# One attention head of sixteen: turned by TensorE in place of VectorE and GpSimd

## The chip, the cores and the metric

The kernel runs on one core of a Trainium2 chip. The core has a matrix engine (TensorE, PE in the profile; its weight loads are PEld), a vector engine (VectorE, DVE), a scalar engine (ScalarE, ACT), GpSimd (POOL) and a queue engine that issues the transfers (SyncE, SP). Each runs its own instruction stream in order and waits for the others through semaphores. SBUF is the on-chip memory of 128 partitions; PSUM is the small memory that TensorE writes to. The metric is the device time of one execution in microseconds, taken as the median of several runs.

## The reference

Two layers work on 256 tokens of 2048 features in float32. Each layer has a mixing part and a gated MLP with a three-tap convolution. The mixing part makes one large projection of the normalised input, which yields queries, keys and values of two attention mixers and two gates. Mixer A is a windowed attention with 8 query heads and 2 key/value heads and a sink logit per head; mixer B is a neighbourhood attention of 8 heads with a learned bias. Cut to what matters here:

```python
qa, ka, va, qb, kb, vb, ga, gb = split_cols(h @ w_in[l])
qa = rotary_partial(rmsnorm(qa.reshape(B, S, HA, HEAD_DIM), qn_a[l]), pos)
...
s = jnp.einsum('bnqgrd,bnkgd->bgrnqk', qb, kw) * (HEAD_DIM ** -0.5)
...
p = jnp.exp(s - m)
p = p / (jnp.sum(p, axis=-1, keepdims=True) + jnp.exp(snk - m))
o = jnp.einsum('bgrnqk,bnkgd->bnqgrd', p, vw)
```

For every head the kernel holds the probabilities `p` with queries on the partitions (two tiles of 128 queries by 256 keys). The product with the values needs keys on the partitions, so each head's 256 x 256 matrix has to be turned before it.

## The kernel before

**The weight stream.** All weights come in units of 16 blocks of 128 x 128 (1 MB), in an order written out by hand (`block_stream`). Every weight is split into a rounded high half, a cast by ScalarE (L338), and the rest as a low half, a subtraction by VectorE (L339); the activations are split likewise, and TensorE multiplies high by high, high by low and low by high. In the token-major projection that runs here (`tokens`, L456 to L458) a unit holds 24 matmuls of 512 columns. Units come through four raw SBUF buffers, which they share with the weights of the adaLN products (L241, on VectorE), and four half-unit buffers `hl`.

**The background.** After each unit a tick runs (`Stream.tick`, `Paced.tick`): first what was deferred, then the paced jobs. One of these is the attention (`attention`, L972), which in layer 1, the second layer, takes 0.4 steps per tick (`ATT`). A step takes each live head one `yield` further, oldest first, and then starts the next head.

**A head.** `attend` (L712) issues, from one step to the next: scores on TensorE (L718) and softmax (VectorE L721 to L736, ScalarE L730 and L738); the turn; the split of the turned matrix `pT` into high (ScalarE, L473) and low (VectorE, L476); and the product with the values (L758) with its own split into `oA` (L761, L762). A turn is made in one of two ways. *Moved*: VectorE transposes the 32 x 32 blocks inside `p` into scratch rows (L319), and GpSimd copies the 16 blocks to their places (L313); one step later the split reads `p` from SBUF. The scratch rows of head `i` in mixer A are `qTa[:, i - 1 : i + 1]`, the queries of head `i` and of the head before, already used (L945); head 0 has a spare tile. *By TensorE*: two steps after the softmax four transposes of 128 x 128 go into a PSUM tile `tp` (L747 to L750), and the split reads that in the same step. In the moved form the ScalarE half of the split is pinned behind what stands on ScalarE's queue so far (`held`, L474).

`MOVED[l]` (L96) says which heads are moved: none in layer 0, all eight of each mixer in layer 1.

**Neighbours.** The projection runs in nine groups of 512 columns. After a group come the squares of its heads (ScalarE, L643), VectorE's sum (L526), a small power on GpSimd (`rsqrt`, L527, the tile `qrs`), and VectorE's product (L653, the tile `qn`), which in layer 1 is pinned in VectorE's queue (`pinned`). One tick later the rows are turned (`turn`): groups 0, 1, 2 and 8 in the moved way (`MOVED_QK`), the others by eight TensorE transposes (L689) into two PSUM tiles `qtp`, which ScalarE empties (L690). Groups 3 and 6 are the keys of mixer B, 5 and 8 its queries.

**PSUM.** `qtp`, `sc` (scores), `tp`, `po` (product with the values) and two rarer tiles share the pool `ax` of three buffers, in turn; the projections have four of their own.

**Order.** Inside an engine the instructions stand in the order in which the tile framework's planner puts them, by program order and by readiness in its own model; `keep_in_program_order` pins one behind those traced before it.

Of the kernel before, what the change touches and what calls it, by code (L numbers as in the profile page):

```python
# [28 lines left out]
SCALE = HEAD ** -0.5  # L29
# [63 lines left out]

MOVED_QK = [(), (0,1,2,8)]
QK_STEPS = 3
MOVED = [(0,0), (8,8)]  # L96
STEPS = [1, 1]

ADA_ORDER = [[p * KC + k for k in range(KC) for p in ps] for ps in ((0, 1), (2,), (3, 4), (5,))]
# [58 lines left out]
def encoder(ctx: ExitStack, tc: tile.TileContext, a: dict, out: bass.AP):  # L158
# [38 lines left out]
    def place(tag, n, dt, name):  # L197
        return sp.tile([P, n, S], dt, name=name, tag=tag)

    def chunks_of(p, tag, room, name, n):  # L200

        t = p.tile([P, room, 2, S], F32R, name=name, tag=tag)
        return [t[:, i] for i in range(n)]
# [5 lines left out]
    def paired(dt, name):  # L209

        return ev.tile([P, 2, S], dt, name=name, tag="u", bufs=2)[:]
# [487 lines left out]
    def in_halves(src, name, tag, yes):  # L699

        if not yes:
            return (src,)
        hl = at.tile([P, 2 * S], F32R, name=name, tag=tag, bufs=1)[:]
        halves = hl.rearrange("p (i s) -> p i s", i=2) if len(src.shape) == 2 else hl.rearrange("p (i a s) -> p i a s", i=2, a=2)
        split(halves, src)
        return halves[:, 0], halves[:, 1]
# [150 lines left out]
    tables = []  # L857

    def small(l):

        if l == 0:
            tables.append(load(a["maskA"], [P, 2, S], "maskA"))
        once = at.tile([P, 2, S], F32, name=f"once{l}", tag="p", bufs=3)[:, 0]
        cs = once[:, : 4 * HALF].rearrange("p (f t d) -> p f t d", f=2, t=2)
        rg = once[:, 4 * HALF : 8 * HALF].rearrange("p (w d) -> p w d", w=2)
        nc.sync.dma_start(cs, a["cs"])
        nc.sync.dma_start(rg, a["rg"][l])
        gains = load(a["gains"][l], [P, 4], f"gains{l}", lay, tag="gains", bufs=1)
        sink = load(a["sink"][l], [P, HA], f"sink{l}", lay, tag="sink", bufs=1)
        nc.vector.tensor_scalar(out=gains[:, 2:3], in0=gains[:, 2:3], scalar1=SCALE, scalar2=None, op0=ALU.mult)  # L870
        rots = []
        for w in range(2):
            rot = lay.tile([P, 4, 2, HALF], F32, name=f"rot{l}_{w}", tag=f"rot{w}", bufs=1)
            for i, (f, g) in enumerate(((0, 0), (1, 1), (0, 1), (1, 0))):
                nc.vector.tensor_tensor(
                    out=rot[:, i], in0=cs[:, f],
                    in1=rg[:, w, g * HALF : (g + 1) * HALF].unsqueeze(1).broadcast_to([P, 2, HALF]), op=ALU.mult,
                )
            rots.append(rot)

        return gains, sink, rots

    for l in range(L):
# [39 lines left out]
        oA, oB = [], []  # L923

        def head_a(i):
            g = i // (HA // GA)
            if i >= 6:
                oA.append(paired(F32R, f"oA{l}_{i}"))
            elif i % 2 == 0:
                o = place(("y0", "y1", "y2")[i // 2], 4, F32R, f"oA{l}_{i}")  # L930
                oA.extend((o[:, :2], o[:, 2:]))
            q = in_halves(qTa[:, i], f"qA{l}_{i}", "qh", l in SCORES_3)
            if i % (HA // GA) == 0:
                kvs[0] = in_halves(kTa[:, g], f"kA{l}_{g}", "kh", l in SCORES_3)
            k = kvs[0]
            yield
            p = at.tile([P, 2, S], F32, name="p", tag="p", bufs=3)

            def v():
                if i % (HA // GA) == 0:  # L940
                    kvs[1] = in_halves(packs[0][:, 1:4:2, g * HEAD : (g + 1) * HEAD], f"vA{l}_{g}", "vh", True)
                return kvs[1]

            def rows():
                return qTa[:, i - 1 : i + 1] if i else paired(F32, f"spare{l}")  # L945

            yield from attend(
                q, k, v, p, tables[0], SCALE, sink[:, i : i + 1], lambda: oA[i], rows if i < MOVED[l][0] else None
            )

        def head_b(hb):
            b, i = packs[1 + hb // 4], hb % 4
            v = b[:, 4:8].rearrange("p (t a) s -> p t (a s)", t=2)
            p = at.tile([P, 2, S], F32, name="p", tag="p", bufs=3)
            nc.sync.dma_start(p[:], a["bias"][l, hb])
            q = in_halves(b[:, 8 + i], f"qB{l}_{hb}", "qh", l in SCORES_3)
            k = in_halves(b[:, i], f"kB{l}_{hb}", "kh", l in SCORES_3)
            yield
            yield from attend(
                q, k, lambda: in_halves(v[:, :, i * HEAD : (i + 1) * HEAD], f"vB{l}_{hb}", "vh", True), p, p, 1.0, None,  # L960
                lambda: oB_of(hb), (lambda: b[:, i : 9 + i : 8]) if hb < MOVED[l][1] else None,
            )

        def oB_of(hb):
            if hb == 0:
                o = place("a", 12, F32R, f"oB{l}_{hb}")
                oB.extend(o[:, 2 * i : 2 * i + 2] for i in range(6))
            elif hb == 6:
                oB.extend(chunks_of(sp, "b0", 6, f"oB{l}_{hb}", 2))
            return oB[hb]  # L970

        def attention():  # L972

            todo = [(EARLY[l] + i // 4, head_a, i) if l in EARLY else (3, head_a, i) for i in range(HA)] + [(6 + 3 * (i // 4), head_b, i) for i in range(HB)]
            live = []
            while todo or live:
                for head in list(live):
                    if next(head, bg) is bg:
                        live.remove(head)
                        heads[0] += 1  # L980
                if todo and ready[0] >= todo[0][0]:
                    live.append(todo[0][1](todo[0][2]))
                    next(live[-1])
                    todo.pop(0)
                yield
# [19 lines left out]
        for pi, (groups, gates) in enumerate(parts):  # L1005
            last = pi == len(parts) - 1
            for g, part in enumerate(groups):
                have_h(part)
                pss = st.tokens(h, part)
                if pi == max(0, len(parts) - 2) and g == 0:  # L1010
                    gains, sink, rots = small(l)
                dst = packs[g // 3][:, 4 * (g % 3) : 4 * (g % 3) + 4]
                rows = dst.rearrange("p (t a) s -> p t a s", t=2)
# [311 lines left out]
```

## Time and profile before

| what | us |
|---|---|
| median of 3 runs | 2582.84 |
| lowest and highest run | 2577.52, 2583.45 |
| the profiled execution | 2582.28 |
| its span in the profile | 2580.4 |
| TensorE busy in the span | 2542.0 |
| VectorE busy | 2206.3 |
| ScalarE busy | 1452.9 |
| GpSimd busy | 243.5 |

The span runs from the first to the last instruction of the profiled execution; 1.9 us of that execution lie around it. A row of the timeline gives the start and the length in microseconds, the engine, the line, the operation, the tile written and the tiles read, the shapes, and in brackets the idle time of that engine just before and what ended it. A row of the stretches gives the stretch, its length, the busy time and the number of instructions of PE, PEld, DVE, ACT and POOL, then the clock granted to TensorE (1.00 is full), the share of the DMA engines' time and GB/s. The chain of work follows the last instruction back, at each step to what released it; its rows in order of time hold start, length, engine, tile and line.

In the second layer the moved turns lie between 1382 and 1695 us, the only long stretch in which GpSimd has work.

### The profile page before, as it was taken

The numbers are of one execution on the slowest core, as the hardware profiler recorded it, in microseconds if no ns is written. First come the engines' busy times: TensorE is split into PE (matmuls) and PEld (weight loads), VectorE is DVE, ScalarE is ACT, GpSimd is POOL, SyncE is SP. The second block draws the span as 40 slices with busy tenths as digits, with TensorE's granted clock in tenths as the row PEclk, the third lists the DMA queues.
The fourth block names the chain that finished last, engine by engine and source line by source line (L and its number), as shares of the span: only waits on it lengthen the run. The fifth ranks groups of instructions, "written<-read, shape, count | busy, mean of one in ns | idle before, by whom it ended". The sixth has DMA issues, their size and how long they took to land.

```text
span 2580.4 us, 41173 instructions
## 1 busy us (share of the span) xinstructions
PE 2542.0 (99%) x16204; PEld 2343.3 (91%) x16204; DVE 2206.3 (85%) x3177; ACT 1452.9 (56%) x2400; POOL 243.5 (9%) x345
## 2 busy tenths in 40 slices
PE   8999999999999999999999989999999999999999
PEld 7888888899999999999998879999999999999998
DVE  8999998998998899899987778879889987766775
ACT  5445865446654665466565666644576546644663
POOL 0000100000000000000004668710000000000000
PEclk9999999999999999999999999999999999999999
DMA  9998689885788778777767667779847775555554
GB/s 364 356 348 308 256 326 359 338 302 217 267 292 308 259 279 299 288 279 280 284 222 275 259 228 267 274 275 332 302 173 293 292 293 198 207 199 197 206 201 147
DMA packets 102149, 699.84 MB, mean 271 GB/s; under 512 B 12865, under 2 KB 15169, under 8 KB 18113
## 3 DMA queue, kind: packets, MB, share of 16 engines
q1 hardware_dynamic: 101954, 697.20, 72.6%
q8 instruction: 127, 2.08, 0.3%
q14 instruction: 68, 0.56, 0.1%
HBM read 695.06 MB, written 2.10 MB: 270 GB/s over the span
## 4 chain that ended last, share of the span: by engine, by line
PE 75%; DVE 14%; DMA 3%; issue 3%; ACT 3%; POOL 2%; DVEq 0%; POOLq 0%; ACTq 0%; SPq 0%
PE ps L381 31%; PE ps L382 15%; DVE hl L339 5%; PE ps_t L457 5%; PE ps_t L458 5%; PE ps_t L456 5%; PE ps L387 4%; PE ps L385 4%; PE ps L386 4%; DVE aw L241 4%; DMA aw<-in_aw 3%; POOL packA L313 1%; ACT hl L338 1%; PE sc L718 1%; DVE x L1137 1%
## 5 line engine op out<-in xcount | busy, mean ns | idle before, releaser
L339 DVE TENSOR_TENSOR hl<-w,hl 128x1024 fp32r<-128x1024 f32 x928 | 1129.2, 1224 | 231.0 <-ACT hl L338 228.6
L338 ACT CAST hl<-w 128x1024 fp32r<-128x1024 f32 x928 | 965.8, 1049 | 583.0 <-PE ps L382 262.0
L381 PE MATMUL ps<-h,hl 128*128 128x512 f32 x2432 | 796.8, 382 | 0.0
L382 PE MATMUL ps<-h,hl 128*128 128x256 f32 x2432 | 663.1, 273 | 0.0
L381 PEld LDWEIGHTS ps<-h,hl 128*128 128x128 f32 x2432 | 460.2, 189 | 63.6
L382 PEld LDWEIGHTS ps<-h,hl 128*128 128x128 f32 x2432 | 467.6, 192 | 0.0
L241 DVE CUSTOM_DVE_ANT_0 aw<-aw,cact,ab 128x2048 f32<-128x2048 f32 x189 | 443.8, 2349 | 15.2 <-DMA aw<-in_aw 14.6
L457 PE MATMUL ps_t<-hl,h 128*128 128x512 f32 x832 | 318.6, 383 | 6.1 <-DVE hl L339 5.9
L456 PE MATMUL ps_t<-hl,h 128*128 128x512 f32 x832 | 315.3, 384 | 4.8 <-ACT hl L338 2.5
L458 PE MATMUL ps_t<-hl,h 128*128 128x512 f32 x832 | 316.6, 381 | 0.0
L457 PEld LDWEIGHTS ps_t<-hl,h 128*128 128x128 f32 x832 | 158.2, 190 | 32.7 <-DVE hl L339 11.2
L456 PEld LDWEIGHTS ps_t<-hl,h 128*128 128x128 f32 x832 | 157.6, 190 | 29.2 <-ACT hl L338 4.5
L458 PEld LDWEIGHTS ps_t<-hl,h 128*128 128x128 f32 x832 | 158.3, 190 | 22.0
L381 PE MATMUL ps<-act_o,hl 128*128 128x512 f32 x512 | 170.5, 382 | 0.0
L1164 DVE SCALAR_TENSOR_TENSOR u<-both,cw,u 128x255 f32<-128x255 f32 x304 | 146.0, 480 | 3.8
L387 PE MATMUL ps<-merged,hl 128*128 128x256 f32 x512 | 141.0, 276 | 6.4 <-DVE hl L339 6.4
L385 PE MATMUL ps<-merged,hl 128*128 128x256 f32 x512 | 141.0, 276 | 0.8 <-ACT hl L338 0.5
L386 PE MATMUL ps<-merged,hl 128*128 128x256 f32 x512 | 140.8, 275 | 0.0
L382 PE MATMUL ps<-act_o,hl 128*128 128x256 f32 x512 | 139.6, 273 | 0.0
L1186 ACT COPY both<-ps 128x256 f32<-128x256 f32 x152 | 56.3, 371 | 123.8 <-PE ps L382 122.8
L1137 DVE SCALAR_TENSOR_TENSOR x<-ps,mod,x 128x256 f32<-128x256 f32 x224 | 105.0, 480 | 21.6 <-PE ps L382 19.5
L381 PE MATMUL ps<-act_y,hl 128*128 128x512 f32 x352 | 118.3, 382 | 0.0
(266 smaller groups left out, 4632.4 us busy)
## 6 DMA issues: line engine op xcount, KB each, us to landing
w<-in_ws SPq DMA_DIRECT2D x463, 1024.0 KB, 4.9
aw<-in_aw SPq DMA_DIRECT2D x189, 1024.0 KB, 4.9
p<-in_bias SPq DMA_DIRECT2D x16, 256.0 KB, 4.4
x<-in_xT SPq DMA_DIRECT2D x4, 512.0 KB, 5.6
aw_o<-in_aw SPq DMA_DIRECT2D x2, 1024.0 KB, 12.4
out<-x SPq DMA_DIRECT2D x16, 128.0 KB, 2.5
w<-in_ws SPq DMA_DIRECT2D x2, 512.0 KB, 11.8
aw_b<-in_aw SPq DMA_DIRECT2D x1, 1024.0 KB, 18.1
```

The costliest lines, as they stand in the source:

```text
L241: product = nc.vector.tensor_tensor_reduce(out=raw[:], in0=raw[:], in1=cact[:], scale=1.0, scalar=ab[:, i : i + 1], op0=ALU.mult, op1=ALU. ...
L338: nc.scalar.copy(hl[:, 0], r)
L339: nc.vector.tensor_tensor(out=hl[:, 1], in0=r, in1=hl[:, 0].bitcast(F32), op=ALU.subtract)
L381: nc.tensor.matmul(ps[:], hi, act.both, start=first, stop=False)
L382: nc.tensor.matmul(ps[:, :S], lo, act.high, start=False, stop=last)
L385: nc.tensor.matmul(out, hi, act[0], start=first, stop=False)
L386: nc.tensor.matmul(ps[:, :S], hi, act[1], start=False, stop=False)
L387: nc.tensor.matmul(out, lo, act[0], start=False, stop=last)
L456: nc.tensor.matmul(ps[:], xh, hi, start=kc == kcs[0], stop=False)
L457: nc.tensor.matmul(ps[:], xh, lo, start=False, stop=False)
L458: nc.tensor.matmul(ps[:], xl, hi, start=False, stop=kc == kcs[-1])
L1164: nc.vector.scalar_tensor_tensor(out=u[:, to], in0=ps[:, of], scalar=w[:, j : j + 1], in1=u[:, to], op0=ALU.mult, op1=ALU.add)
```

## The change

The bound "the first n heads" becomes a set of heads for each layer and mixer, and head index 2 of mixer A is not in layer 1's set:

```diff
-MOVED = [(0,0), (8,8)]
+MOVED = [((), ()), ((0, 1, 3, 4, 5, 6, 7), range(8))]
...
-                q, k, v, p, tables[0], SCALE, sink[:, i : i + 1], lambda: oA[i], rows if i < MOVED[l][0] else None
+                q, k, v, p, tables[0], SCALE, sink[:, i : i + 1], lambda: oA[i], rows if i in MOVED[l][0] else None
...
-                lambda: oB_of(hb), (lambda: b[:, i : 9 + i : 8]) if hb < MOVED[l][1] else None,
+                lambda: oB_of(hb), (lambda: b[:, i : 9 + i : 8]) if hb in MOVED[l][1] else None,
```

That head then takes the other branch of `attend`, which layer 0 takes for all its heads:

```python
        yield
        if rows is not None:
            turned_blocks(p[:], rows(), 2)
            for _ in range(STEPS[sink is None]):
                yield
            tp = p
        else:
            yield
            tp = ax.tile([P, 2, S], F32, name="tp", tag="ax")
            for k in range(2):
                for t in range(2):
                    nc.tensor.transpose(tp[:, k, t * P : (t + 1) * P], p[:, t, k * P : (k + 1) * P], ident[:])
        pT = at.tile([P, 2, 2, S], F32R, name="pT", tag="pT", bufs=1)
        split(pT, tp[:], held=rows is not None)
```

## The prediction

> **What bounds the kernel now.** I read the page's head first, for the span and the busy shares, and then the chain's shares by engine.
>
> ```profile
> span 2580.4 us, 41173 instructions
> PE 2542.0 (99%) x16204; PEld 2343.3 (91%) x16204; DVE 2206.3 (85%) x3177; ACT 1452.9 (56%) x2400; POOL 243.5 (9%) x345
> PE 75%; DVE 14%; DMA 3%; issue 3%; ACT 3%; POOL 2%; DVEq 0%; POOLq 0%; ACTq 0%; SPq 0%
> ```
>
> TensorE is busy for 2542.0 of 2580.4 us, so it is the bound, and only 38.4 us of it are idle. An edit off TensorE pays only where one of those gaps closes; an edit that adds TensorE work costs its full length wherever there is no gap. The next view is the stretches around the third head, with TensorE's busy time as the second number and the granted clock (PEclk) as the third from the end.
>
> ```profile
> 1480.00:1500.00 20.00, 17.22 (x86) 14.96 (x85) 11.42 (x13) 10.90 (x29) 14.58 (x26) 1.00 0.55 211
> 1500.00:1520.00 20.00, 15.70 (x75) 13.57 (x74) 16.14 (x33) 14.02 (x40) 10.26 (x21) 0.91 0.57 211
> 1520.00:1540.00 20.00, 20.00 (x104) 17.76 (x103) 16.83 (x25) 12.41 (x21) 10.42 (x16) 1.00 0.72 263
> ```
>
> From 1480 to 1520 us TensorE is idle for 2.78 + 4.30 = 7.08 us, almost a fifth of its idle time in the whole program, and the clock falls. From 1520 on it is full. The third head is turned exactly here. TensorE's timeline (start, length, and in brackets the idle time before it) and the chain in order of time say which work is late:
>
> ```profile
> 1498.93 0.48 PE L457 MATMUL ps_t<-hl,h 128*128 128x512 f32 x1 [2.78 <-DVE hl L339]
> 1504.00 1.04 PE L689 MATMUL qtp<-ident,qn 128*128 128x128 f32 x8
> 1504.79 0.91 PE L758 MATMUL po<-pT,vA 128*128 128x256 f32 x6
> 1510.23 1.23 PE L718 MATMUL sc<-kA,qA 128*128 128x256 f32 x6 [4.30 <-ACT packB L690]
> ```
> ```profile
> 1510.23 1.23 PE sc L718 x6
> 1511.46 0.43 PE ps_t L457
> ...
> 1514.02 0.34 PE ps_t L457
> ...
> 1528.84 0.67 PE sc L718 x6
> 1534.69 0.87 PE qtp L689 x8
> ```
>
> The first gap waits for VectorE's low halves of a weight unit (L339), the second for ScalarE to empty the PSUM tiles of group 5's turned queries (L690). After the second gap the same six score matmuls take 1.23 us where they take 0.67 a step later, and the seven matmuls from 1511.46 to 1514.36 (1514.02 + 0.34) take 2.90 us where seven of 0.22 take 1.54. That is 0.56 + 1.36 = 1.92 us lost to the clock.
>
> Why are VectorE and ScalarE late? VectorE, GpSimd and ScalarE, in this order:
>
> ```profile
> 1483.96 0.71 DVE L319 STREAM_TRANSPOSE packA<-p 128x512 f32<-128x512 f32 x1 [2.50 <-POOL p L313]
> 1488.01 0.25 DVE L526 TENSOR_SCALAR qss<-qss 128x8 f32<-128x8 f32 x1
> 1496.46 1.29 DVE L653 TENSOR_TENSOR qn<-ps_t,qrs 128x512 f32<-128x512 f32 x2 [5.85 <-POOL qrs L527]
> 1499.93 0.42 DVE L762 TENSOR_TENSOR oA<-po,oA 128x256 fp32r<-128x256 f32 x1
> 1505.89 0.16 DVE L736 RECIPROCAL ri<-den 128x2 f32<-128x2 f32 x1
> ```
> ```profile
> 1475.59 8.34 POOL L313 COPY p<-packA 32x128 f32<-32x128 f32 x16 [5.84 <-DVE packA L319]
> 1484.74 9.97 POOL L313 COPY p<-packA 32x128 f32<-32x128 f32 x16 [0.81 <-DVE packA L319]
> 1494.79 1.64 POOL L527 TENSOR_TENSOR qrs<-qss,mhalf 128x8 f32<-128x8 f32 x1
> ```
> ```profile
> 1481.57 1.03 ACT L338 CAST hl<-w 128x1024 fp32r<-128x1024 f32 x1
> 1490.62 1.99 ACT L338 CAST hl<-w 128x1024 fp32r<-128x1024 f32 x2 [3.87 <-DVE hl L339]
> 1502.20 0.51 ACT L730 ACTIVATE p<-p,nm 128x256 f32<-128x256 f32 x1 [7.24 <-DVE nm L727]
> 1506.14 0.91 ACT L738 ACTIVATE p<-p,ri 128x256 f32<-128x256 f32 x2 [1.71 <-DVE ri L736]
> 1509.48 1.27 ACT L690 ACTIVATE packB<-qtp,gains 128x512 f32<-128x512 f32 x2
> ```
>
> The transpose at 1483.96 is the third head's. Its scratch (rows 1 and 2 of the mixer-A queries) overlaps the second head's (rows 0 and 1), so VectorE stands 2.50 us until GpSimd has copied the second head. Then GpSimd copies the third head until 1494.71, and the small power for group 5's norm (qrs), whose input was ready at 1488.26, runs only at 1494.79. VectorE's next instruction, the norm's product pinned in its queue, waits 5.85 us for it, with the L339 of the next unit behind it: that is TensorE's first gap. The attention's row maxima are late too, ScalarE waits 7.24 and 1.71 us for VectorE, and its L690, late by as much, makes the second gap. Both gaps begin at the third head's move.
>
> **The change, part by part.** Only head index 2 of layer index 1 leaves the moved set; `range(8)` covers the same mixer-B heads as `< 8`, and layer 0 stays empty.
>
> Removed: one VectorE transpose (0.71 us, with its 2.50 us wait) and 16 GpSimd copies (9.97 us). Then the power for group 5 finds GpSimd free at 1483.93. VectorE passes the transpose's place some 2.5 + 0.7 us sooner, less 1.1 us until ScalarE's cast of 1481.57 is done, so everything moves up by about 2 us: the sums are ready near 1486.3, the power near 1488.0, the casts of 1490.62 start near 1488.7. Product (1.3) and L339 pair (2.5) follow at 1488.7 to 1492.5 instead of 1496.46 to 1500.01. TensorE wants that unit at 1496.15 (1498.93 - 2.78): **the first gap closes**, with 3 us to spare. What is late next: from the output half at 1499.93 to the reciprocal at 1505.89 VectorE needs 5.96 us without a hole, so it comes to 1492.5 + 6.0 = 1498.5. ScalarE's normalisation and one cast (0.9 + 1.0) end near 1500.5. TensorE ends group 6 at 1504.00 - 2.78 = 1501.2, so ScalarE is there in time, by less than 1 us.
>
> Added: four TensorE transposes, one ScalarE cast and one VectorE subtraction from PSUM in place of the same two from SBUF, and a PSUM tile (`tp`) in a pool of three. Layer 0 turns all its heads so:
>
> ```profile
> 277.20 0.60 PE L750 MATMUL tp<-ident,p 128*128 128x128 f32 x4
> 281.08 1.29 PE L718 MATMUL sc<-packA 128*128 128x256 f32 x4 [2.42 <-ACT packB L690]
> 288.72 0.60 PE L750 MATMUL tp<-ident,p 128*128 128x128 f32 x4
> 289.16 1.03 PE L718 MATMUL sc<-packA 128*128 128x256 f32 x4
> ```
> ```profile
> L473 ACT CAST pT<-tp x16: 563/586/592, 283.1 to 444.5; 128x512 fp32r<-128x512 f32 x16
> L476 DVE TENSOR_TENSOR pT<-tp,pT x16: 668/682/693, 283.8 to 445.1; 128x512 fp32r<-128x512 f32 x16
> L473 ACT CAST pT<-p x16: 618/626/645, 1469.8 to 1705.9; 128x512 fp32r<-128x512 f32 x16
> L476 DVE TENSOR_TENSOR pT<-p,pT x16: 677/765/777, 1471.7 to 1707.2; 128x512 fp32r<-128x512 f32 x16
> ```
>
> From 288.72 to 289.16 the four take 0.44 us, as do half of the eight in 0.87 above. Nothing hides it: 0.44 us. The two split instructions become 0.04 and 0.08 us shorter, off the path: nothing. The pT cast is no longer pinned on ScalarE; I cost that at nothing, since it needs `tp` and cannot go ahead of it.
>
> The new wait is the PSUM tile. The loops put the turn two attention steps after the softmax, at the unit's end where group 5's two `qtp` tiles, the second head's `po`, then `tp`, then the fifth head's scores are all issued. With three buffers, `tp` waits for the first L690 and the scores for the second; behind them stand the token matmuls. No row shows this mix in layer 1. The bounds are 0 and layer 0's 2.42 us for the same pair L690 to scores. From group 6's end ScalarE has two squares (0.7 us), a cast (1.0) and the two L690 (0.6 each) to do, so these end 2.3 and 2.9 us after it; TensorE has 0.87 of qtp, 0.67 of po, one matmul of 0.22 and 0.44 of tp, so about 0.8 us stay open. I take 0.8.
>
> The clock: does a short wait lose it? Layer 0 again, as two windows:
>
> ```profile
> 280.00:282.00 2.00, 0.92 (x5) 0.84 (x5) 2.00 (x4) 1.94 (x8) 0.00 (x0) 0.98 0.65 254
> 282.00:284.00 2.00, 2.00 (x6) 1.53 (x6) 2.00 (x6) 1.97 (x8) 0.00 (x0) 0.50 0.51 139
> ```
>
> The 2.42 us gap there, with twelve transposes just ahead, was followed by half clock, while the 2.78 us gap here, with none ahead, was not: the full rate is back at 1498.93. For 0.8 us I count no loss; 1.92 us is kept as the other end. [...]
>
> Sum: 2.78 + 4.30 + 1.92 - 0.44 - 0.80 = 7.76 us. The profiled execution took 2582.28 us, 0.56 under the median of 2582.84: 2582.28 - 7.76 = **2574.5 us**.
>
> **Rivals.** *The PSUM pool takes half of it back*: the wait is layer 0's 2.42 us and the clock falls after it. Gain 2.78 + 4.30 + 1.92 - 0.44 - 2.42 - 1.92 = 4.2, so 2578.1 us. For: the same tiles in layer 0. Against: there ScalarE did a softmax between the turn and L690. *Only the clock stays lost*, since twelve transposes stand side by side with 0.8 us of idle: 7.76 - 1.92 = 5.8, so 2576.4 us. For: the two gaps above. [...] *The gap only moves*: the other heads still go through GpSimd, and the next power (group 6) may be late behind the fourth head's copies, or VectorE's backlog of 5.96 us be late anyway. Then only the first gap goes: 2.78 - 0.44 = 2.3, so 2579.9 us. Against: TensorE is full from 1520 on with the same copies beside it.
>
> *Slower*: TensorE's queue stands at `tp` until L690, and the cast that PE needs next stands on ScalarE behind a pT cast that itself waits for `tp`. Each such round costs what the second gap costs today, 4.30 + 1.92 = 6.2 us. One round leaves 2582.28 - 9.0 + 0.44 + 6.2 = 2579.9; the change is slower by 0.3% from three rounds on (18.6 us, 2592.3 us), if the order of the later steps shifts as well. For: the order within an engine is the planner's and may change downstream. Against: TensorE is full from 1520 on, so the later steps have room.
>
> **Numbers.** About 0.3% (7.7 us, to 2575.1) is what a measurement of this kernel can tell from no change. The forecast has 0.50, of which 0.04 may come out above that line; more than the two gaps (a better order later on) 0.04; the pool 0.17, the clock 0.10, the moved gap 0.12, slower 0.07. So faster 0.50, same 0.43, slower 0.07. The range runs from 2569 (the whole 9.0 - 0.44 gained, and the scatter of the runs, 2577.52 to 2583.45) to 2581.5, which takes in the pool, the clock and the moved gap.
>
> **What would show it.** Right: VectorE without the 2.50 and 5.85 us waits, qrs at about 1488, L690 near 1503, TensorE's idle time from 1480 to 1520 below 1.5 us and PEclk 1.00 throughout. Wrong: a wait of `tp` or `sc` for L690 above 2 us, PEclk 0.5 after it, or new waits of TensorE for L339 after 1520.

## The result, and the profile after

| | before | after |
|---|---|---|
| median, us | 2582.05 (6 runs) | 2572.42 (6 runs) |
| lowest and highest | 2577.52, 2583.45 | 2570.09, 2574.32 |
| ratio, 95% interval | | 0.9972 [0.9962, 0.9982] |
| span of the profiled execution | 2580.4 | 2570.7 |

The kernel became faster. The medians differ by 9.6 us, the ratio by 0.28%, or 7.2 us; the interval, 4.6 to 9.8 us, holds both. The head of the page and the stretches that the prediction showed, now after the change:

```profile
span 2570.7 us, 41162 instructions
PE 2540.1 (99%) x16208; PEld 2340.9 (91%) x16208; DVE 2205.8 (86%) x3176; ACT 1453.0 (57%) x2400; POOL 239.8 (9%) x329
```
```profile
1480.00:1500.00 20.00, 20.00 (x105) 17.75 (x104) 17.40 (x26) 12.97 (x31) 8.27 (x8) 1.00 0.68 268
1500.00:1520.00 20.00, 18.50 (x97) 16.14 (x96) 15.59 (x23) 13.67 (x36) 17.62 (x30) 1.00 0.69 261
1520.00:1540.00 20.00, 20.00 (x106) 17.81 (x105) 17.41 (x31) 14.31 (x30) 12.04 (x19) 1.00 0.68 235
```

GpSimd has 16 instructions less, VectorE one less, TensorE four more. TensorE stood idle for 7.08 us from 1480 to 1520; now it is 1.50 us, and the granted clock stays at 1.00. TensorE's timeline shows where the 1.50 us are:

```profile
1498.91 1.04 PE L689 MATMUL qtp<-ident,qn 128*128 128x128 f32 x8
1499.71 0.91 PE L758 MATMUL po<-pT,vA 128*128 128x256 f32 x6
1502.34 0.66 PE L750 MATMUL tp<-ident,p 128*128 128x128 f32 x4 [1.50 <-ACT packB L690]
1502.91 0.94 PE L718 MATMUL sc<-kA,qA 128*128 128x256 f32 x6
```

**A yardstick of its own.** Executions differ by a few microseconds in the first layer: the first head's scores of the second layer start at 1444.03 us before and at 1441.85 after, though TensorE's order is the same up to the fourth head's scores. They differ behind the change, too: from the sixth head's scores to the end of the span it is 1051.0 us after and 1053.3 us in e11, the same kernel run again. So whole times can't weigh one microsecond. I use the stretch from the start of the fourth head's scores to the start of the sixth head's scores (L718), which holds both gaps: 1489.92 to 1528.67 = **38.75 us before**, 1487.88 to 1519.68 = **31.80 us after**. The change took 6.95 us out of it. Of the 9.7 us between the two spans 2.04 lie ahead of the stretch and 0.71 behind it.

VectorE, GpSimd and ScalarE after the change, the rows that answer to those of the prediction:

```profile
1484.05 0.25 DVE L526 TENSOR_SCALAR qss<-qss 128x8 f32<-128x8 f32 x1
1488.56 1.29 DVE L653 TENSOR_TENSOR qn<-ps_t,qrs 128x512 f32<-128x512 f32 x2 [1.91 <-POOL qrs L527]
1489.77 2.35 DVE L339 TENSOR_TENSOR hl<-w,hl 128x1024 fp32r<-128x1024 f32 x2
1497.99 0.16 DVE L736 RECIPROCAL ri<-den 128x2 f32<-128x2 f32 x1
```
```profile
1473.55 13.26 POOL L313 COPY p<-packA 32x128 f32<-32x128 f32 x16 [5.84 <-DVE packA L319]
1486.89 1.63 POOL L527 TENSOR_TENSOR qrs<-qss,mhalf 128x8 f32<-128x8 f32 x1
```
```profile
1494.31 0.51 ACT L730 ACTIVATE p<-p,nm 128x256 f32<-128x256 f32 x1 [1.92 <-DVE nm L727]
1498.25 0.91 ACT L738 ACTIVATE p<-p,ri 128x256 f32<-128x256 f32 x2 [1.71 <-DVE ri L736]
1499.07 1.03 ACT L338 CAST hl<-w 128x1024 fp32r<-128x1024 f32 x1
1500.66 1.04 ACT L338 CAST hl<-w 128x1024 fp32r<-128x1024 f32 x1
1501.59 1.27 ACT L690 ACTIVATE packB<-qtp,gains 128x512 f32<-128x512 f32 x2
```

The 2.50 us wait for the scratch rows is gone, the wait for the power (qrs) is 1.91 in place of 5.85 us, and ScalarE waits 1.92 in place of 7.24 us. But GpSimd needs 13.26 us for the second head's 16 copies, where it needed 8.34, and so the power starts 2.59 us after its sums are ready (1486.89 - 1484.30). Why the same copies became slower is read in the trace of before. Of its chain, the copies of the second head one by one, and then VectorE's L339 beside them:

```profile
1475.59 1.20 POOL p L313
...
1476.83 0.28 POOL p L313
...
1477.97 1.25 POOL p L313
...
1479.27 0.28 POOL p L313
...
1480.25 1.36 POOL p L313
```
```profile
1475.45 1.18 DVE L339 TENSOR_TENSOR hl<-w,hl 128x1024 fp32r<-128x1024 f32 x1
...
1477.86 1.21 DVE L339 TENSOR_TENSOR hl<-w,hl 128x1024 fp32r<-128x1024 f32 x1
...
1480.24 1.23 DVE L339 TENSOR_TENSOR hl<-w,hl 128x1024 fp32r<-128x1024 f32 x1 [0.48 <-ACT hl L338]
```

A copy takes 0.28 us, but one that meets an L339 takes 1.20 to 1.36 us: it ends about when the L339 ends (1476.79 and 1476.63, 1479.22 and 1479.07, 1481.61 and 1481.47). While VectorE stood 2.50 us for the scratch, the copies from 1481.66 on took 0.26 to 0.30 us each. Once VectorE works on, they take longer: after the change three more L339 (one at 1480.59, two from 1484.21 on) and an L241 of 2.38 us (at 1481.74) fall into the time of the same 16 copies, and the copies of 1480.60 and 1482.01 took 1.37 and 2.26 us.

### The profile page after: what moved, and what is told of

Read it like the earlier page. It is cut to its first block, busy times and chain, and to the rows that moved or that the text cites. A ratio compares the mean times of both kernels' runs of the same rounds, so it can differ in the third digit from the quotient of the medians.

```text
span 2570.7 us, 41162 instructions
## 1 busy us (share of the span) xinstructions
PE 2540.1 (99%) x16208; PEld 2340.9 (91%) x16208; DVE 2205.8 (86%) x3176; ACT 1453.0 (57%) x2400; POOL 239.8 (9%) x329
## 4 chain that ended last, share of the span: by engine, by line
PE 75%; DVE 14%; issue 3%; ACT 3%; DMA 3%; POOL 2%; DVEq 0%; ACTq 0%; POOLq 0%
PE ps L381 31%; PE ps L382 16%; DVE hl L339 5%; PE ps L387 5%; PE ps L385 4%; PE ps L386 4%; PE ps_t L457 4%; PE ps_t L458 4%; PE ps_t L456 4%; DVE aw L241 4%; DMA aw<-in_aw 2%; ACT hl L338 1%; POOL packA L313 1%; POOL p L313 1%; DVE x L1137 1%
## 5 line engine op out<-in xcount | busy, mean ns | idle before, releaser
L339 DVE TENSOR_TENSOR hl<-w,hl 128x1024 fp32r<-128x1024 f32 x928 | 1130.1, 1226 | 233.9 <-ACT hl L338 231.8
L241 DVE CUSTOM_DVE_ANT_0 aw<-aw,cact,ab 128x2048 f32<-128x2048 f32 x189 | 444.2, 2351 | 12.1 <-DMA aw<-in_aw 12.0
```

The costliest lines, as they stand in the source:

```text
L241: product = nc.vector.tensor_tensor_reduce(out=raw[:], in0=raw[:], in1=cact[:], scale=1.0, scalar=ab[:, i : i + 1], op0=ALU.mult, op1=ALU. ...
L339: nc.vector.tensor_tensor(out=hl[:, 1], in0=r, in1=hl[:, 0].bitcast(F32), op=ALU.subtract)
```

## The experiments

All eleven are measured by the stretch, "4th to 6th" below. The single times are one execution each. Beside e1 to e4 the kernel before took 2583.29 us, beside e5 to e8 2582.27 (one execution each), beside e9 to e11 2580.94 (median of 18).

| run | 4th scores | 6th scores | 4th to 6th, us | time, us |
|---|---|---|---|---|
| before | 1489.92 | 1528.67 | 38.75 | 2582.05 |
| after | 1487.88 | 1519.68 | 31.80 | 2572.42 |
| e1 copies kept | 1486.69 | 1525.87 | 39.18 | 2576.45 |
| e2 transpose kept | 1488.40 | 1520.38 | 31.98 | 2574.32 |
| e3 before, own scratch | 1489.98 | 1527.99 | 38.01 | 2582.76 |
| e4 fifth head instead | 1491.30 | 1528.37 | 37.07 | 2581.47 |
| e5 qtp one unit later | 1488.50 | 1518.39 | 29.89 | 2570.55 |
| e6 second head too | 1488.44 | 1518.79 | 30.35 | 2573.03 |
| e7 cast pinned | 1489.01 | 1520.80 | 31.79 | 2574.24 |
| e8 all of mixer A | 1489.18 | 1519.89 | 30.71 | 2575.59 |
| e9 before, qtp later | 1488.12 | 1522.28 | 34.16 | 2575.79 (10 runs) |
| e10 as e5, timed | 1487.13 | 1517.03 | 29.90 | 2571.86 (5 runs) |
| e11 the change again | 1489.98 | 1521.78 | 31.80 | 2572.96 (8 runs) |

### Which of the removed parts cost the time: e1, e2, e3

e1 adds 16 copies to the changed kernel at the old place; they go to a tile that nothing reads:

```diff
+            def copies(src):
+                spare = paired(F32, f"dup{l}")
+                blocks = src.rearrange("p t (n k) -> p n t k", n=2)
+                dst = spare.rearrange("p t (n k) -> p (t n k)", n=2).rearrange("p (n t k) -> p n t k", n=2, t=2)
+                moved_blocks(dst, blocks)
...
         else:
+            if extra is not None:
+                extra(p[:])
             yield
```

> The third head is turned by TensorE as in the changed kernel, and GpSimd still copies 16 blocks of its matrix at the old place, into a tile that nobody reads. Measure: TensorE's time from the start of the fourth head's scores to the start of the sixth head's scores (38.75 us before, 31.80 us after the change). Theory (what cost time is GpSimd's queue, with group 5's power behind the copies): the power runs only after the copies, VectorE waits 6 us or more for it, both TensorE gaps return, 37 to 41 us. Rival (VectorE's own transpose and its wait for the scratch rows cost the time): 32 to 33 us.

GpSimd's queue, VectorE's product behind it, and TensorE's waits in e1:

```profile
1472.36 13.25 POOL L313 COPY p<-packA 32x128 f32<-32x128 f32 x16 [5.85 <-DVE packA L319]
1485.67 5.22 POOL L313 COPY dup<-p 32x128 f32<-32x128 f32 x16
1490.97 1.64 POOL L527 TENSOR_TENSOR qrs<-qss,mhalf 128x8 f32<-128x8 f32 x1
```
```profile
1492.64 1.29 DVE L653 TENSOR_TENSOR qn<-ps_t,qrs 128x512 f32<-128x512 f32 x2 [7.18 <-POOL qrs L527]
```
```profile
PE tp L752 <- ACT packB L690: 4.3, 1, 4.3
PE ps_t L457 <- DVE hl L339: 2.4, 2, 2.2
```

The copies alone bring back both gaps, 2.2 and 4.3 us, and 39.18 us. The whole time of this one execution does not come back with them: its span is 5.7 us shorter than that of before, 3.2 us of it ahead of the stretch and 2.9 us behind it, while the stretch is 0.4 us longer. The run also shows the price of a copy from both sides: sixteen take 5.22 us where VectorE stands, 13.25 us where it works.

e2 adds only VectorE's transpose into the old scratch rows.

```diff
+                (lambda src: nc.vector.transpose(out=rows(), in_=src)) if l == 1 and i == 2 else None
```

> The third head is turned by TensorE, and VectorE still transposes its blocks into the old scratch rows, which nobody reads; GpSimd copies nothing for it. Theory (GpSimd's queue): VectorE waits some 2 to 5 us for the second head's copies, but the power starts right after those, the first TensorE gap stays away, and the stretch between the fourth and the sixth head's scores is 32 to 34 us. Rival (the scratch wait): 37 us or more.

VectorE's waits, and GpSimd's queue, in e2:

```profile
DVE packA L951 <- POOL p L313: 2.5, 1, 2.5
...
DVE qn L653 <- POOL qrs L527: 0.4, 1, 0.4
```
```profile
1474.07 8.34 POOL L313 COPY p<-packA 32x128 f32<-32x128 f32 x16 [5.86 <-DVE packA L319]
1486.75 2.47 POOL L527 TENSOR_TENSOR qrs<-qss,mhalf 128x8 f32<-128x8 f32 x1 [4.35 <-DVE qss L526]
```

The scratch wait of 2.5 us is back and costs TensorE 0.18 us, which is its longer wait at `tp` (1.68 us). The copies are again done in 8.34 us, because VectorE stands, but its sums come 1.8 us later against the fourth head's scores, and the power takes 2.47 us: it is done 0.82 us after the start of the fourth head's scores (1486.75 + 2.47 - 1488.40), after the change 0.64 us.

e3 leaves the kernel before as it was and gives the third head a scratch tile of its own.

```diff
-                return qTa[:, i - 1 : i + 1] if i else paired(F32, f"spare{l}")
+                return qTa[:, i - 1 : i + 1] if i not in (0, 2) else paired(F32, f"spare{l}_{i}")
```

> The kernel before, with a scratch tile of its own for the third head in place of the query rows that overlap the second head's. Theory (GpSimd's queue): VectorE no longer waits for the rows, but the power still stands behind 16 copies and these run no faster; the stretch stays at 37 to 39 us with both gaps. Rival (the scratch wait begins the delay): the 2.50 us wait goes, and the stretch falls to 36 us or less.

GpSimd's queue and VectorE's wait for the power in e3:

```profile
1475.65 13.26 POOL L313 COPY p<-packA 32x128 f32<-32x128 f32 x16 [5.85 <-DVE packA L319]
1488.96 5.25 POOL L313 COPY p<-spare 32x128 f32<-32x128 f32 x16
1494.30 1.64 POOL L527 TENSOR_TENSOR qrs<-qss,mhalf 128x8 f32<-128x8 f32 x1
```
```profile
DVE qn L653 <- POOL qrs L527: 7.2, 1, 7.2
```

The scratch wait is gone, yet the power starts at 1494.30 where it started at 1494.79: what VectorE saves in front, it waits behind. TensorE's gaps are 2.23 and 2.62 us, and the clock falls behind both (0.50 from 1500 to 1502 and from 1510 to 1512). Together the three say that the third head's *copies*, ahead of a power that is needed at once, cost the time, and not VectorE's transpose or its wait. No run puts the power ahead of the copies in GpSimd's queue or frees VectorE's pinned product; that the lateness takes this way is read from the rows.

### The place, not the engine: e4, e8, and e7 for the pin

```diff
-MOVED = [((), ()), ((0, 1, 3, 4, 5, 6, 7), range(8))]
+MOVED = [((), ()), ((0, 1, 2, 3, 5, 6, 7), range(8))]    (e4)
+MOVED = [((), ()), ((), range(8))]                       (e8)
```

> The fifth head of mixer A is turned by TensorE in place of the third. Theory (it is the place of the copies just ahead of group 5's power, not the engine that turns): the stretch between the fourth and the sixth head's scores stays at 38 to 39 us with both gaps, and the later part costs four transposes, 0.4 us, more: a time within 2 us of the kernel before. Rival (any head that leaves GpSimd is worth it): several us faster than before.

Both gaps stayed, 2.78 and 2.81 us. The second was shorter than before and the stretch, 37.07 us, fell below the expected 38: half clock behind the first gap (0.50 from 1500 to 1503) brought TensorE to the second 1.5 us later, the scores behind it still start 20.31 us after the fourth head's (1511.61 - 1491.30, before 1510.23 - 1489.92), and from there the clock stays full (1.00 from 1511 to 1518). The time is within 1 us of before's median and 1.8 us below the execution of before beside it.

> All eight heads of mixer A in the second layer are turned by TensorE. Theory (only a turn ahead of a power that is needed soon pays; each of the seven others costs four transposes, 0.44 us): beside the changed kernel the stretch is 31 to 32.5 us and the whole some 2 to 4 us longer, 2574 to 2577 us. Rival (every head off GpSimd pays): 2570 us or less.

2575.59 us lie in the range of the theory, 3.2 us above the changed kernel's median, but this is one execution, so what the seven other heads cost or gain is not shown by it. The stretch came out below its range, 30.71 us, since the power is free of all copies as in e6.

e7 pins the cast in the changed kernel:

```diff
-        split(pT, tp[:], held=rows is not None)
+        split(pT, tp[:], held=True)
```

> The changed kernel, with ScalarE's cast of the turned third head pinned in its queue, as it was before the change. Theory (the pin is worth nothing here): the stretch stays within 0.3 us of 31.80. Rival (part of the gain comes from the freed order on ScalarE): 32.5 us or more.

31.79 us: the pin is worth nothing here.

### What is left of the gap: e5, e6, e9, e10; and e11, the change again

e5 defers the turn of group 5 in layer 1 by one more tick; for the other groups one tick remains.

```diff
-            bg.defer(lambda: turn(qn))
+            later(wait + 1, lambda: turn(qn))
...
-                    qk_rows(pss, 4, None, ..., dst, turned, g in MOVED_QK[l], l == 1)
+                    qk_rows(pss, 4, None, ..., dst, turned, g in MOVED_QK[l], l == 1, int(l == 1 and g == 5))
```

> The changed kernel, with the turn of group 5's queries (the two qtp tiles) one unit later, so that it no longer shares its moment with po, tp and the scores. Theory (the 1.50 us that TensorE still waits at tp are the PSUM pool's three buffers): the wait goes, and the stretch from the fourth to the sixth head's scores falls from 31.80 to about 30.3 us. Rival (ScalarE is late whatever the tiles): qtp or the scores wait in place of tp, and the stretch stays at 31.5 us or more.

The stretches of e5:

```profile
1480.00:1500.00 20.00, 20.00 (x103) 17.72 (x102) 16.93 (x27) 12.98 (x33) 8.77 (x9) 1.00 0.70 265
1500.00:1520.00 20.00, 20.00 (x111) 17.91 (x110) 16.22 (x25) 14.99 (x38) 18.26 (x29) 1.00 0.66 251
```

TensorE has no hole left, and the stretch is 29.89 us, 1.91 less than after the change and 0.4 below the expected 30.3. With the tiles apart, TensorE does not wait: three buffers for `qtp`, `qtp`, `po`, `tp` and the scores were the new wait.

e6 turns the second head (index 1) by TensorE, too:

```diff
-MOVED = [((), ()), ((0, 1, 3, 4, 5, 6, 7), range(8))]
+MOVED = [((), ()), ((0, 3, 4, 5, 6, 7), range(8))]
```

> The changed kernel, with the second head of mixer A turned by TensorE as well. Theory (the rest of the delay is the second head's copies, 13.26 us beside a busy VectorE, ahead of the power): VectorE's 1.91 us wait for the power goes, ScalarE reaches L690 earlier by 1 us or more, tp waits 0.5 us or less, and the stretch falls to 30.3 to 30.8 us, while the added transposes cost 0.44 us ahead of it. Rival (ScalarE's own order before L690 sets the wait): tp still waits 1.2 us or more.

VectorE's wait for the power falls to 0.4 us, the power starts at once,

```profile
1484.25 2.47 POOL L527 TENSOR_TENSOR qrs<-qss,mhalf 128x8 f32<-128x8 f32 x1 [16.36 <-DVE qss L526]
```

and the matmuls of `tp` no longer wait: 30.35 us. Only the weight loads of `tp` and of the scores still wait for L690, 0.3 and 0.2 us, and the stretch is 0.46 us longer than in e5. So the 1.50 us have two conditions, five tiles in three buffers and a ScalarE that is late because of the second head's copies; removing the first takes the wait away, removing the second nearly so.

e9 makes e5's edit in the kernel before.

> The kernel before (the third head still goes through VectorE and GpSimd), with the two qtp tiles of group 5 one unit later. Theory (the second gap is VectorE's and ScalarE's lateness reaching TensorE through the PSUM pool alone): the first gap of 2.2 to 2.8 us stays, the second, 4.30 us, goes with its clock loss, and the stretch from the fourth to the sixth head's scores falls from 38.75 to 32.5 to 33.5 us; about 6 us faster than the kernel before. Rival (the lateness reaches TensorE by the weights anyway): a new wait for L339 of 2 us or more, and 35 us or more.

TensorE's waits in e9, and the row at the end of the one that is left:

```profile
PE ps_t L457 <- DVE hl L339: 2.8, 1, 2.8
```
```profile
1497.13 0.79 PE L457 MATMUL ps_t<-hl,h 128*128 128x512 f32 x1 [2.78 <-DVE hl L339]
```

The second gap of 4.30 us is gone with all the copies in place, the first stays. ScalarE and VectorE are as late as before (7.23 us of waiting for the row maxima), and TensorE does not feel it: the second gap came through the PSUM pool. (Half clock behind the first gap, 0.92 on the mean from 1492 to 1514, holds TensorE back by 1.6 us here, so a wait shorter than that on another way would not show.) The stretch is 34.16 us, above the 33.5 expected, because the first gap was followed by half clock here (the matmul at its end takes 0.79 us, before 0.48). The time is 0.9977 [0.9967, 0.9986] of before, 5.9 us.

e10 is the kernel of e5, in five executions.

> The changed kernel with group 5's qtp tiles one unit later, timed. Theory: about 1.9 us faster than the changed kernel beside it, so some 9 us faster than the kernel before, ratio 0.9965. Rival (given back later): no faster than the changed kernel, ratio 0.9972 or more.

0.9962 [0.9949, 0.9974], and the stretch is again 29.90 us. By the stretch this is the best of the versions, 1.9 us ahead of the changed kernel; by the whole time the two intervals overlap, so the whole time does not tell them apart.

e11 is the changed kernel once more, in eight executions.

> The changed kernel once more, to see how much of the 9.6 us between the medians is its own. Theory (the two profiles differ by 6.95 us between the fourth and the sixth head's scores, and by some 2 us ahead of the first touched instruction, which is scatter of the executions): ratio 0.9970 to 0.9974, about 7 us. Rival (the whole 9.6 us): 0.9963 or less.

0.9972 [0.9962, 0.9983] and 31.80 us, as in the first measurement. The stretch says that the change is worth some 7 us. The ratio is the one expected, but its interval just takes in the rival's 0.9963, and the medians here differ by 8.0 us, so whole times alone do not exclude the 9.6. The first head's scores start at 1444.02 us here, where they started at 1441.85, with the same kernel.

## Why the prediction was right, point by point

**The first gap** (2.78 us) closed, as predicted, and by the step that was named: the copies off GpSimd's queue ahead of the power. e1 and e3 show it. The power was expected at about 1488.0 less the 2 us by which this execution is ahead in all, 1486.0 done; it was done at 1488.52 (1486.89 + 1.63), and the L339 pair ended at 1492.12 where 1490.5 was expected. TensorE had 3 us of room, and this took none of its time.

**The second gap** (4.30 us) became 1.50 us; the prediction left 0.80. (Its own terms, 2.9 less 2.2 us, leave 0.70.) This is the term that was mis-sized, and the cause is the step "the power finds GpSimd free at 1483.93": it took the second head's 8.34 us over into a kernel in which VectorE no longer stands beside them. They took 13.26 us. VectorE came to the reciprocal at 1497.99 rather than 1496.5, ScalarE's cast ended at 1500.10 when TensorE had ended group 6 at 1498.91. So `tp` started 3.4 us after group 6 (1502.34 - 1498.91), where the first L690 was planned to end 2.3 us after it; the room of "less than 1 us" was not there. e6 removes those copies, and with them one transpose on VectorE, and the matmuls of `tp` stop waiting.

**The clock** (1.92 us) came back: 1.00 throughout. The prediction counted no loss for a short wait, and that held at 1.50 us; the reason it weighed did not hold. The prediction weighed that transposes in front of a gap might decide whether the clock falls: that was its author's estimate, from two gaps alone (2.42 us behind twelve transposes, then 0.50; 2.78 us behind none, then 1.00). The experiments have gaps of both kinds. In e3 and e4, TensorE's rows with the gap in brackets, and the clock just behind them:

```profile
1498.44 0.48 PE L457 MATMUL ps_t<-hl,h 128*128 128x512 f32 x1 [2.23 <-DVE hl L339]
...
1509.74 1.65 PE L718 MATMUL sc<-kA,qA 128*128 128x256 f32 x6 [2.62 <-ACT packB L690]
```
```profile
1499.00:1502.00 3.00, 3.00 (x9) 2.42 (x8) 3.00 (x11) 0.29 (x1) 0.00 (x0) 0.53 0.33 109
```
```profile
1500.31 0.79 PE L457 MATMUL ps_t<-hl,h 128*128 128x512 f32 x1 [2.78 <-DVE hl L339]
...
1511.61 0.94 PE L718 MATMUL sc<-kA,qA 128*128 128x256 f32 x6 [2.81 <-ACT packB L690]
```
```profile
1500.00:1503.00 3.00, 2.69 (x6) 2.18 (x7) 3.00 (x7) 0.00 (x0) 0.00 (x0) 0.50 0.15 38
1511.00:1515.00 4.00, 3.39 (x19) 3.08 (x20) 3.63 (x9) 3.87 (x16) 3.67 (x9) 1.00 0.85 313
```

A gap of 2.23 us with no transposes ahead of it cost clock; one of 2.81 us behind eight transposes and seven matmuls cost none, one of 2.62 us behind the same work in e3 did; and 2.78 us cost clock in e4 and none in the kernel before. So in these traces neither the transposes nor the length within 2.2 to 2.8 us tells the cases apart.

Where the gap falls does. In before from 100 us on, and in e3 and e4 from 1492 to 1518, the granted clock changed only at points that lie whole multiples of 3.41 us apart: in e3 at 1499.17, 1502.58, 1509.41 and 1512.82 us (3.41, 2 x 3.41 and 3.41 apart), in e4 at 1499.95 and 1503.36, in before at 281.93, 285.34, 1510.72 and 1514.14 us (the middle two 359 x 3.413 apart) and at 2579.10. The table takes these steps of 3.41 us as a grid; that of after is counted back from 2571.02 us, the only change in its trace. Each half clock in the table lasted one step. The idle time is the step's length less TensorE's busy time in it:

| trace | grid step, us | TensorE idle in it, us | clock in the next step |
|---|---|---|---|
| before, layer 0 | 278.51 to 281.93 | 2.42 | 0.50 |
| before, first gap | 1493.66 to 1497.07 | 0.92 | 1.00 |
| before, first gap | 1497.07 to 1500.49 | 1.86 | 1.00 |
| before, second gap | 1507.31 to 1510.72 | 2.92 | 0.50 |
| e3, first gap | 1495.76 to 1499.17 | 2.23 | 0.50 |
| e3, second gap | 1506.00 to 1509.41 | 2.29 | 0.50 |
| e4, first gap | 1496.54 to 1499.95 | 2.42 | 0.50 |
| e4, second gap | 1506.78 to 1510.19 | 1.39 | 1.00 |
| e4, second gap | 1510.19 to 1513.60 | 1.42 | 1.00 |
| after, wait of `tp` | 1499.24 to 1502.65 | 1.50 | 1.00 |

The first gap of before (0.92 and 1.86 us) and the second of e4 (1.39 and 1.42 us) have the end of a step inside them and kept the clock, which is luck of the execution; the 1.50 us after the change stay below every idle time in the table that cost clock. In the whole traces of before and after, from 100 us on, the three steps followed by half clock, all in before, held 2.42, 2.92 and 2.51 us of idle time (the last from 2575.68 on); no other held more than 1.86 us (before) and 1.72 us (after). Where between 1.86 and 2.23 us the clock begins to fall these rows do not show, nor why it falls. The idle time here counts transposes as work; without them the step of after would have 2.28 us of it (1.50, and 0.78 of `qtp` and `tp`), more than the 2.23 us that cost clock in e3, and its clock stayed at 1.00.

**The added work** (0.44 us) was not measured by itself; in the rows of after, 0.57 us pass from the start of `tp` to that of the scores, and 0.36 us in e5, where TensorE does not wait. Put together, 9.00 - 0.44 - 1.50 = 7.06 us, and the stretch lost 6.95, so no larger term is missing.

**The rivals.** The PSUM pool did take back part, 1.50 us of the 2.42 that layer 0 shows, and without the clock. The gap did not move elsewhere, TensorE is full from 1520 to 1540 as before. The slower case, a pT cast in front of the casts that TensorE needs, did not occur, and e7 shows that pinning this cast changes nothing.

**The number.** 2574.5 us was predicted for one execution of before at 2582.28; 2572.42 and 2572.96 us were measured, inside the range of 2569 to 2581.5. The distance of 2 us is of the size by which executions differ ahead of the change, so that it is no larger is luck in part. By the stretch the gain was 6.95 us where 7.76 were forecast, and most of the 0.8 us between them is the wait at `tp`. Two of the signs were met in part only: TensorE's idle time from 1480 to 1520 is 1.50 us, not below it, and VectorE still waits 1.91 us for the power. By the prediction's own line of 0.3% between faster and same the ratio (0.28%) lies just under it and the medians (0.37%) above it.

## What to carry to other kernels

Look at what is queued behind a batch on a side engine: 16 copies cost nothing that shows on the fifth head (e4) and 7 us on the third, because a 1.6 us instruction that a bound engine needs soon stood behind them. Before moving work to the matrix engine, ask which PSUM buffer the new tile takes and who empties it; moving the neighbour by one step (e5, 1.91 us of the stretch) was worth more than the second removal (e6, 1.45 us). When a stall on one engine is removed, the engine that ran beside it may slow down (here the second head's copies, from 8.34 to 13.26 us), so don't carry its durations over.

## What was not expected of the hardware

Twelve of GpSimd's 16 block copies of the second head took 0.26 to 0.30 us in before, but one that met an L339 of 1.18 to 1.23 us on VectorE took 1.20 to 1.36 us, and one that met the L241 of 2.38 us took 2.26 us (after). Sixteen took 5.22 us (e1, VectorE standing) to 13.26 us (after, VectorE working), and 8.34 us with VectorE standing part of the time (before). What holds the copies up is not shown; they end 0.14 to 0.16 us after those L339.

TensorE's granted clock changed at points whole multiples of 3.41 us apart (before, e3, e4). It was 0.50 in the steps behind 2.23 to 2.92 us of idle time and 1.00 in those behind 1.86 us or less, in the rows of the table, so a gap of 2.78 us cost clock in e4 and none in the kernel before, as the steps divided it.
